# Hybrid conformer and forgetting-attention layer on one core: scores pinned behind maxima in TensorE's order, bias rows stored once, value loads apart, later roots in parts, second block first

## The chip, the cores and the metric

One NeuronCore of a Trainium2 chip runs the whole layer in one launch. The metric is the device time of that launch in microseconds. The engines are TensorE (PE), VectorE (DVE), ScalarE (ACT), GpSimd (POOL) and SyncE (SP), which here issues most of the DMA transfers; POOL issues the others. Each engine takes its own instructions in the order in which the program has them, so an instruction that waits holds up those behind it on its engine.

## The reference

One encoder layer with D_MODEL 1024 for 2048 prompt frames and 8 streams of 16 sample frames; all in float32. Heads are 8 of 64 channels, the convolution group has 512 channels, the FFN 2816.

```python
def _mixer_inputs(x, shift, scale, norm1_g, w_in, b_f, q_norm_g, k_norm_g):
    h = _rmsnorm(x, norm1_g) * (1 + scale) + shift
    u_a, u_g, q, k, v, f = jnp.split(h @ w_in, [...], axis=-1)
    u = u_a * jax.nn.sigmoid(u_g)
    # q and k: RMS norm of each head
    logf = jax.nn.log_sigmoid((f + b_f).astype(jnp.float32))
    return u, q, k, v, logf

def _attend(q, k, v, cum_q, cum_k, q_pos, k_pos):
    s = jnp.einsum('bqhd,bkhd->bhqk', q, k) * (HEAD_DIM ** -0.5)
    s = s + (cum_q[..., :, None] - cum_k[..., None, :])
    s = jnp.where(k_pos[None, :] <= q_pos[:, None], s, NEG_INF)
    p = jax.nn.softmax(s, axis=-1)
    return jnp.einsum('bhqk,bkhd->bqhd', p, v)

def _layer(x, c, past, ...):
    sh1, sc1, g1, sh2, sc2, g2 = _modulation(c, w_ada, b_ada)
    u, q, k, v, logf = _mixer_inputs(x, sh1, sc1, ...)
    # prompt: causal attention; sample: over 1024 cached frames and its own 16
    conv_out = _conv_module(u_hist, conv_w, conv_b, ln_g, ln_b)   # depthwise 31, LayerNorm, swish
    mix = jnp.concatenate([conv_out, attn], axis=-1) @ w_out
    x = x + g1 * mix
    h = _rmsnorm(x, norm2_g) * (1 + sc2) + sh2
    x = x + g2 * ((jax.nn.silu(h @ w_gate) * (h @ w_up)) @ w_down)
    return x, (k, v, logf, new_conv)
```

## The kernel before

Matrix products run as three passes: each operand is split into a rounded part (`hi`, a copy on ACT) and the rest (`lo`, a subtraction on DVE or POOL); `parts_of` does that at lines 1149 and 1150. The stages follow each other, with work of neighbouring stages woven in:

- *Start, 0 to about 120 us.* Modulation (`ada`), then blocks of 384 frames through the input projection. `h_block` loads a block's x, squares it on ACT, makes the root of its mean square (`pr`, L455), and yields the normalised, split `hx` piece by piece. `project_u_v` does the first block while weights `Wu` arrive, then loads and splits the eight pieces of `Wv` (`wraw`, `wvh`, `wvl`), and only after them starts `h_block` of the second block. `pg` and `pa` are the gated products, `pvv` the values.
- *Projection of q and k, to about 600 us*, beside the convolution's taps on DVE. `finish` norms each block (`ssq`, `R`, `qn`, `qp`) and writes `q_d` and `k_d`.
- *Attention, about 600 to 1225 us.* 16 steps, for each of 4 head pairs p and 4 query blocks qb of 512. A step is cut into pieces: 128 keys by up to 512 queries of one head; there are 320 in all. `score_maxima` makes the row maxima beforehand: a matmul `mx` (L927) into one of two `cv` banks, and a reduction `M` on DVE (L930); when a step's maxima are made, `spread_maxima` puts them as extra rows into `Q2`, and it does so after the fourth maximum of the step that follows. `attend` computes each piece's scores `s` (L966, L967) with these rows, the exponential `ef` and its copy `e` on ACT, the subtraction for `e` on DVE (on POOL every third time), and the matmuls `pv` with the values some pieces later. `ef` is a ring of three tiles; `load` takes one of them for a value block `vraw`, which ACT and DVE split into `V`. `load(0)` stands ahead of the first step. `K1`, `K2` are rings of six tiles, `Q2` of four. Beside the steps `background` runs the convolution's LayerNorm (`lane`, `cy`) and the attention of the sample streams.
- *Sample streams.* `sample_setup` makes a bias row of 1040 for each of 64 (stream, head) pairs and stores it 16 times over, once for each query, in `bias_d`; `sample_batch` loads a stream's 128 rows into `S`.
- *Output projection, to 1434 us* (`acc`, L1133), and the *FFN* (`z`, L1440), three pairs of frame blocks by a fast matrix multiplication with seven products of sub-blocks (`sums`, `right_sides`). The first pair's norm lies in `project_out`; those of the second and third are made by `norms` during the first pair of `ffn_up`, one step of the generator for each `q` from the second pair of columns (`f`) on. `root` holds matmuls `pr` (L1229), a chain of small Newton steps on DVE, diagonals `odg` (L1237), matmuls with them (L1238) and a copy to `oR` on ACT.

The order of instructions on each engine is set by a scheduler, which simulates the program and picks by readiness and priority. `weave` sets the order in which a step's parts are handed to it, and `after` binds one instruction behind another of the same engine without a wait:

```python
    def after(self, ins, last):
        self.tc.add_manual_dep(
            ins.ins, last.ins.name,
            mybir.DependencyInfo(mybir.DependencyClass.NoSync, mybir.DependencyReason.DATA), reason="order")
```

## Time and profile before

| | us |
|---|---|
| median of 3 runs (lowest to highest) | 2842.85 (2842.31 to 2846.67) |
| the profiled execution | 2842.93 |
| its span, first to last instruction | 2841.2 |
| PE busy | 2729.4 |
| DVE busy | 2160.8 |
| ACT busy | 1435.3 |
| POOL busy | 506.0 |

In the rows that follow, a table of stretches gives for each its bounds, its length, the busy time of the engines with the number of instructions, the granted TensorE clock as a share of full speed, the DMA engines' share and GB/s. A row of a group gives line, engine, operation, output<-input, shapes and count, then busy us and mean ns, then the engine's idle time just before these instructions and what ended it. A row of a timeline gives start and duration, and in brackets the idle time before it and what ended it. A row of the chain gives start, duration and what. A row of DMA issues ends with the KB of one, and the us to its landing where the profile has it. A row that ends in two numbers behind a name tells who waited, for how many us and how often.

### The profile page before, as it was taken

Reading aid. Unit: us, or ns where it says so; the run is one execution under the profiler, and the core shown is the slowest. Engines: PE = TensorE matmul, PEld = TensorE weight load, DVE = VectorE, ACT = ScalarE, POOL = GpSimd, SP = SyncE. Lnnn points to the kernel's source line nnn. Section 1 sums busy time; section 2 is a strip of 40 time slices with the busy share of each in tenths; the row PEclk is TensorE's granted clock in tenths of the full one; section 3 lists DMA queues with packets and bytes.
Section 4 is the critical chain, followed back from the end, with each engine's and each line's share of the span. In section 5 each row is a group of like instructions: output and inputs, shape, how many; then the busy total and the mean of one; then the engine's idle time right before and its main releaser. Section 6 shows DMA issues by size and latency. Waiting matters only on the chain.

```text
span 2841.2 us, 48479 instructions
## 1 busy us (share of the span) xinstructions
PE 2729.4 (96%) x16536; PEld 2521.3 (89%) x16536; DVE 2160.8 (76%) x4235; ACT 1435.3 (51%) x2812; POOL 506.0 (18%) x685
## 2 busy tenths in 40 slices
PE   7899999989988999999998999999999999999999
PEld 6899988866666777788998999999999999999999
DVE  3698898988786788635488899777797778676765
ACT  4443323357675777754354455444454446555552
POOL 3454411243232222213202020000000000000000
PEclk9999999988899999999998999999999999999999
DMA  8763567674236656355667678776786669788883
GB/s 306 247 196 113 176 220 255 189 204 124 82 110 175 191 182 185 116 174 189 212 238 232 237 264 287 255 229 208 227 296 213 217 209 310 245 281 257 271 255 117
DMA packets 390024, 603.23 MB, mean 212 GB/s; under 512 B 46240, under 2 KB 249152, under 8 KB 387728
## 3 DMA queue, kind: packets, MB, share of 16 engines
q1 hardware_dynamic: 375312, 574.72, 62.6%
q0 software_dynamic: 14464, 25.42, 3.7%
q8 instruction: 130, 2.13, 0.3%
q14 instruction: 118, 0.97, 0.1%
HBM read 421.97 MB, written 178.07 MB: 211 GB/s over the span
## 4 chain that ended last, share of the span: by engine, by line
PE 78%; DMA 9%; DVE 6%; ACT 3%; issue 3%; POOL 2%; SPq 1%; DVEq 0%; ACTq 0%; POOLq 0%
PE z L1440 44%; PE z L510 7%; PE pv L957 5%; PE acc L1133 4%; PE pa L320 3%; PE pvv L340 3%; PE pg L320 3%; PE s L966 2%; PE s L967 2%; PE mx L927 2%; DMA vraw<-o_v 1%; DVE M L930 1%; DMA wraw<-w_in 1%; DMA k_d<-qp 1%; PE lane L1096 1%
## 5 line engine op out<-in xcount | busy, mean ns | idle before, releaser
L1440 PE MATMUL z<-rT,rW 128*128 128x360 f32 (+1 forms) x8316 | 1382.6, 328 | 5.1 <-ACT oR L1240 1.9
L1440 PEld LDWEIGHTS z<-rT,rW 128*128 128x128 f32 x8316 | 1379.4, 188 | 6.9 <-ACT oR L1240 2.3
L1149 ACT ACTIVATE rW<-rR 128x512 fp32r<-128x512 f32 x714 | 435.1, 617 | 397.9 <-PE z L1440 285.6
L1150 DVE TENSOR_TENSOR rW<-rR,rW 128x512 fp32r<-128x512 f32 x714 | 477.6, 673 | 154.7 <-ACT rW L1149 150.8
L698 DVE SCALAR_TENSOR_TENSOR cv<-cu,cpar,cv 128x384 f32<-128x384 f32 x580 | 311.6, 616 | 2.6 <-ACT cv L696 2.5
L957 PE MATMUL pv<-e,V 128*128 128x512 f32 (+3 forms) x960 | 265.0, 381 | 22.6 <-ACT e L1149 13.1
L957 PEld LDWEIGHTS pv<-e,V 128*128 128x128 f32 x960 | 168.9, 192 | 68.3 <-ACT e L1149 15.2
L930 DVE TENSOR_REDUCE M<-mx 128x1 f32<-128x512 f32 (+2 forms) x320 | 190.1, 605 | 50.5 <-PE mx L927 34.9
L971 ACT ACTIVATE ef<-s 128x512 f32<-128x512 f32 (+3 forms) x320 | 166.0, 529 | 104.8 <-PE s L967 46.7
L510 PE MATMUL z<-hqx,wqh 128*128 128x384 f32 (+1 forms) x768 | 196.6, 333 | 1.3 <-DVE logf L347 1.3
L1149 ACT ACTIVATE rT<-traw 128x360 fp32r<-128x360 f32 (+1 forms) x315 | 149.9, 501 | 88.8 <-DMA traw<-gt_d 52.5
L1150 POOL TENSOR_TENSOR e<-ef,e 128x512 fp32r<-128x512 f32 (+3 forms) x106 | 127.0, 1198 | 364.4 <-ACT e L1149 182.1
L1150 DVE TENSOR_TENSOR rT<-traw,rT 128x360 fp32r<-128x360 f32 (+1 forms) x315 | 158.4, 533 | 41.3 <-ACT rT L1149 41.0
L1150 DVE TENSOR_TENSOR e<-ef,e 128x512 fp32r<-128x512 f32 (+3 forms) x214 | 147.3, 698 | 40.8 <-ACT e L1149 38.1
L1149 ACT ACTIVATE e<-ef 128x512 fp32r<-128x512 f32 (+3 forms) x320 | 174.2, 565 | 4.4
L510 PEld LDWEIGHTS z<-hqx,wqh 128*128 128x128 f32 x768 | 135.7, 188 | 19.2 <-issue 15.5
L927 PE MATMUL mx<-K,Q 96*128 96x512 f32 (+2 forms) x320 | 133.6, 426 | 15.3 <-DVE M L930 13.2
L1133 PE MATMUL acc<-ch,woh 128*128 128x360 f32 (+1 forms) x384 | 128.4, 336 | 9.9 <-ACT ch L1149 5.0
L1368 DVE TENSOR_TENSOR rR<-rR 128x512 f32<-128x512 f32 (+1 forms) x136 | 90.5, 683 | 54.6 <-DMA rR<-w_down 50.0
L966 PE MATMUL s<-Q,K 128*128 128x512 f32 (+3 forms) x320 | 126.7, 397 | 3.2 <-ACT ef L971 3.0
L1133 PE MATMUL acc<-ch,wol 128*128 128x360 f32 (+1 forms) x384 | 128.1, 334 | 0.0
L510 PE MATMUL z<-hqx,wql 128*128 128x384 f32 (+1 forms) x384 | 126.4, 329 | 0.0
(306 smaller groups left out, 3955.5 us busy)
## 6 DMA issues: line engine op xcount, KB each, us to landing
rR<-sup_d SPq DMA_DIRECT2D x176, 256.0 KB
rR<-w_gate SPq DMA_DIRECT2D x132, 256.0 KB
traw<-gt_d SPq DMA_DIRECT2D x154, 180.0 KB
rR<-w_down SPq DMA_DIRECT2D x104, 256.0 KB
rR<-sdn_d SPq DMA_DIRECT2D x96, 256.0 KB
rR<-w_up SPq DMA_DIRECT2D x88, 256.0 KB
sup_d<-rR SPq DMA_DIRECT2D x88, 256.0 KB
wa<-w_ada SPq DMA_DIRECT2D x16, 1024.0 KB
```

The source lines that it names most:

```text
L320: nc.tensor.matmul(pz[:, :n], w[:, m], x[:, :n], start=(c == 0 and k == 0), stop=(c == CB - 1 and k == 2))
L510: nc.tensor.matmul(z[:, :n], w[:, m], x[:, :n], start=(c == 0 and k == 0), stop=(c == CB - 1 and k == 2))
L698: self.pin(nc.vector.scalar_tensor_tensor(dst, src, w, acc[i], ALU.mult, ALU.add))
L927: nc.tensor.matmul(mx[:, :w], Q2[0:AUX, h, j * P:(j + 1) * P], K2[kb][0:AUX, h, :w], start=True, stop=not diag)
L930: nc.vector.tensor_reduce(M[:, i, kb:kb + 1], mx[:, :w], AX.X, ALU.max)
L957: nc.tensor.matmul(z[h][:, off:], V[kt // 4][:, v, kt % 4, h:h + 2, :].rearrange("p b c -> p (b c)"), e[:, x, off:], start=(kt == 0 and i ...
L966: nc.tensor.matmul(s[:, off:], K1[kb][:, h, sl], Q1[:, h, off:], start=True, stop=False)
L971: nc.scalar.activation(ef[:, off:], s[:, off:], AF.Exp)
L1133: self.nc.tensor.matmul(z[:, :n], w[:, m], y, start=(first and i == 0 and k == 0), stop=(last and i == len(terms) - 1 and k == 2))
L1149: self.nc.scalar.activation(hi, raw, AF.Copy)
L1150: engine.tensor_tensor(lo, raw, f32(hi), ALU.subtract)
L1440: nc.tensor.matmul(z, W[:, x, m], t[:, y, :w], start=(k == 0 and i == 0), stop=(k == n - 1 and i == 2))
```

## The change

Five things are changed. (1) Every score piece's first matmul is bound behind the maximum that is 32 to 40 pieces on (32 for the first, one more for every six). (2) `bias_d` holds each row once, and `S` is loaded head by head with the row repeated 16 times by the load. (3) `vraw` has a tile of its own tag `rs`, shared with the reciprocal of a step's end, instead of one of the `ef` ring; `load` yields after its transfer is issued, and the split's copy on ACT is bound behind the last exponential written so far; the first block's load is issued ahead of the steps and split among them. (4) `root` yields twice between the diagonals and their matmuls, and `norms` starts at the third pair of columns. (5) `h_block` of the second block starts ahead of the `Wv` loads.

```diff
-            self.bias_d = d.tile([NS * H, QS, PAST + QS], F32, name="bias_d")
+            self.bias_d = d.tile([NS * H, PAST + QS], F32, name="bias_d")
...
         wvp = ctx.enter_context(self.pool(name="wv", bufs=1))
+        pending = None
+        h1 = self.h_block(*BLOCKS1[1], stage, sp, hp)
+        next(h1)
         Wv = [self.split(wvp, 2 * D, 520, c, "wv", nc.vector) for c in range(CB)]
-        pending = None
-        hs_next = list(self.h_block(*BLOCKS1[1], stage, sp, hp))[2:]
+        hs_next = list(h1)[1:]
...
-        drain(self.load(0))
+        first = self.load(0)
+        next(first)
+        next(first)
...
                 parts.append((self.last_parts(), 12))
+                parts.append((first, 4))
...
-        raw = self.awk.tile([P, 4, P], F32, tag="ef", name="vraw", bufs=3)
+        raw = self.awk.tile([P, 4, P], F32, tag="rs", name="vraw", bufs=1)
         nc.sync.dma_start(raw, self.a["o_v"][t].rearrange("(t p) e -> p t e", p=P)[:, :, p * P:(p + 1) * P])
         v = self.Vt[n % 4]
+        self.V.setdefault(p, []).append(v)
+        yield
         hi, lo = (v[:, i, :, 0:3:2, :] for i in range(2))
-        self.parts_of(hi, lo, raw.rearrange("p t (h e) -> p t h e", h=2), nc.vector)
-        self.V.setdefault(p, []).append(v)
+        self.after(self.parts_of(hi, lo, raw.rearrange("p t (h e) -> p t h e", h=2), nc.vector), self.last_piece)
...
+                    self.mx.append(nc.tensor.matmul(mx[:, :w], Q2[0:AUX, h, j * P:(j + 1) * P], K2[kb][0:AUX, h, :w], start=True, stop=not diag))
...
+                first = nc.tensor.matmul(s[:, off:], K1[kb][:, h, sl], Q1[:, h, off:], start=True, stop=False)
+                at = min(self.nscore + AHEAD + min(self.nscore // 6, 8), len(self.mx) - 1)
+                self.after(first, self.mx[at])
+                self.nscore += 1
...
+                self.last_piece = nc.scalar.activation(ef[:, off:], s[:, off:], AF.Exp)
...
-        nc.sync.dma_start(self.bias_d, bias[:n].unsqueeze(1).broadcast_to([n, QS, PAST + QS]))
+        nc.sync.dma_start(self.bias_d, bias[:n])
...
-        nc.sync.dma_start(S, self.bias_d[b * H:(b + 1) * H].rearrange("h q k -> (h q) k"))
+        for h in range(H):
+            nc.sync.dma_start(S[h * QS:(h + 1) * QS], self.bias_d[b * H + h:b * H + h + 1].broadcast_to([QS, PAST + QS]))
...
-                first.append(self.root(*pending, sp))
+                drain(self.root(*pending, sp, first))
...
+        dg = [sp.tile([P, NW // 4], F32, tag="dg", name="odg", bufs=4)[:m, :m] for _ in range(4)]
         for i in range(4):
-            dg = sp.tile([P, NW // 4], F32, tag="dg", name="odg", bufs=4)[:m, :m]
-            nc.vector.tensor_scalar(dg, ident[:m, :m], r[:, i:i + 1], None, ALU.mult)
-            nc.tensor.matmul(pr[:, i * m:(i + 1) * m], ones[:m], dg, start=True, stop=True)
+            nc.vector.tensor_scalar(dg[i], ident[:m, :m], r[:, i:i + 1], None, ALU.mult)
+        yield
+        yield
+        for i in range(4):
+            nc.tensor.matmul(pr[:, i * m:(i + 1) * m], ones[:m], dg[i], start=True, stop=True)
...
-                R.append(self.root(s, n, pool))
                 yield
+                yield from self.root(s, n, pool, R)
...
-                        if p == 0 and f and u == 0:
+                        if p == 0 and f > 2 and u == 0:
                             next(norms, None)
```

Where this stands in the engines' order. The first place is TensorE at the border of the third and fourth step of the first pair: `mx` are maxima, `s` scores, `pv` matmuls with values, `pz` the transposition ahead of `Q2`'s rows. Before:

```order
L966 MATMUL s<-Q_7802,K_6647 128x512
L957 MATMUL pv<-e,V_7013 128x128
L714 MATMUL lane<-cq,ones 32x512
...
L927 MATMUL mx<-K_6643,Q_6667 128x512
L927 MATMUL mx<-K_6648,Q_6667 128x512
L927 MATMUL mx<-K_6655,Q_6667 128x512
L927 MATMUL mx<-K_6658,Q_6667 128x512
L929 MATMUL mx<-masks 128x128
L927 MATMUL mx<-K_6661,Q_6645 128x128
L929 MATMUL mx<-masks 128x128
...
L941 MATMUL pz<-ident,Z_6636 128x128
```

After, at the same `pz`:

```order
L973 MATMUL s<-Q_7440,K_6657 128x384
L977 MATMUL s<-Q_6653,K_6655 128x384
L979 MATMUL s<-masks 128x128
L964 MATMUL pv<-e,V_7013 128x512 x2
L934 MATMUL mx<-K_6661,Q_6645 128x512
L936 MATMUL mx<-masks 128x128
L973 MATMUL s<-Q_7440,K_6657 128x256
L977 MATMUL s<-Q_6653,K_6655 128x256
L979 MATMUL s<-masks 128x128
L948 MATMUL pz<-ident,Z_6636 128x128
```

Before, 14 maxima stand with no score between them ahead of the transposition that the next step needs; after, a maximum and a score alternate, and the scores that are on are still those of the step before.

The second place is SP's order of transfers around the bias store, before:

```order
L1040 DMA bias_d<-bias 1024x1x1040
L901 DMA vraw<-o_v 128x4x128
L1054 DMA kc<-kcT 128x4x512
L1046 DMA S<-bias_d 128x1040 x2
L1054 DMA kc<-kcT 128x4x512
```

and after:

```order
L1050 DMA bias_d<-bias 64x1040
L1065 DMA kc<-kcT 128x4x512
L1057 DMA S<-bias_d 16x1040 x16
L906 DMA vraw<-o_v 128x4x128
L1006 DMA cat_d<-pvs 128x512
```

The value load `vraw` that stood right behind the store now stands ahead of the whole set-up, and the next one behind the sixteen loads of `S`.

The third place is TensorE in the FFN's first pair, around the roots of the second pair, before:

```order
L1440 MATMUL z<-rT,rW 128x368 x264
L1229 MATMUL pr<-sp_13306,ns 90x2 x4
L1440 MATMUL z<-rT,rW 128x368 x72
L1238 MATMUL pr<-odg,sp_13305 128x90 x4
L1229 MATMUL pr<-sp_13306,ns 90x2 x4
L1238 MATMUL pr<-odg,sp_13305 128x90 x4
L1440 MATMUL z<-rT,rW 128x368 x372
```

and after:

```order
L1456 MATMUL z<-rT,rW 128x368 x372
L1241 MATMUL pr<-sp_13362,ns 90x2 x4
L1456 MATMUL z<-rT,rW 128x368 x134
L1253 MATMUL pr<-odg,sp_13361 128x90 x4
L1456 MATMUL z<-rT,rW 128x368 x46
L1241 MATMUL pr<-sp_13362,ns 90x2 x4
L1456 MATMUL z<-rT,rW 128x368 x72
L1253 MATMUL pr<-odg,sp_13361 128x90 x4
```

The two halves of the second root stood together, with no FFN matmul between; now 134 and 72 stand between the halves.

More of the change, by code (lines that the diff above doesn't have):

```diff
@@ L899, in load @@
         self.Q1[n] = Q1
-        raw = self.awk.tile([P, 4, P], F32, tag="ef", name="vraw", bufs=3)
+        raw = self.awk.tile([P, 4, P], F32, tag="rs", name="vraw", bufs=1)
         nc.sync.dma_start(raw, self.a["o_v"][t].rearrange("(t p) e -> p t e", p=P)[:, :, p * P:(p + 1) * P])
         v = self.Vt[n % 4]
+        self.V.setdefault(p, []).append(v)
+        yield
         hi, lo = (v[:, i, :, 0:3:2, :] for i in range(2))
-        self.parts_of(hi, lo, raw.rearrange("p t (h e) -> p t h e", h=2), nc.vector)
-        self.V.setdefault(p, []).append(v)
+        self.after(self.parts_of(hi, lo, raw.rearrange("p t (h e) -> p t h e", h=2), nc.vector), self.last_piece)
     def score_maxima(self):
         nc = self.nc
+        self.mx, self.nscore = [], 0
         spread = None
@@ L926, in score_maxima @@
                     mx = self.bank("cv", "mx")
-                    nc.tensor.matmul(mx[:, :w], Q2[0:AUX, h, j * P:(j + 1) * P], K2[kb][0:AUX, h, :w], start=True, stop=not diag)
+                    self.mx.append(nc.tensor.matmul(mx[:, :w], Q2[0:AUX, h, j * P:(j + 1) * P], K2[kb][0:AUX, h, :w], start=True, stop=not diag))
                     if diag:
@@ L965, in attend @@
                 s = self.bank("u", "s")
-                nc.tensor.matmul(s[:, off:], K1[kb][:, h, sl], Q1[:, h, off:], start=True, stop=False)
+                first = nc.tensor.matmul(s[:, off:], K1[kb][:, h, sl], Q1[:, h, off:], start=True, stop=False)
+                at = min(self.nscore + AHEAD + min(self.nscore // 6, 8), len(self.mx) - 1)
+                self.after(first, self.mx[at])
+                self.nscore += 1
                 nc.tensor.matmul(s[:, off:], K2[kb][:, h, sl], Q2[:, h, off:], start=False, stop=not diag)
@@ L970, in attend @@
                 ef = wk.tile([P, 512], F32, tag="ef", name="ef", bufs=3)
-                nc.scalar.activation(ef[:, off:], s[:, off:], AF.Exp)
+                self.last_piece = nc.scalar.activation(ef[:, off:], s[:, off:], AF.Exp)
                 pool, tag = self.eslots[self.ecount % len(self.eslots)]
@@ L1147, in parts_of @@
     def parts_of(self, hi, lo, raw, engine):
-        self.nc.scalar.activation(hi, raw, AF.Copy)
+        copy = self.nc.scalar.activation(hi, raw, AF.Copy)
         engine.tensor_tensor(lo, raw, f32(hi), ALU.subtract)
+        return copy
     def split_rows(self, hi, lo, src, ring, tag):
@@ L1221, in project_out, with root @@
                 self.pump()
-    def root(self, ssum, n, sp):
+    def root(self, ssum, n, sp, out):
         nc, (ones, mean, ident) = self.nc, self.spread
@@ L1234, in root @@
         newton_rsqrt(nc, r, t, v, 3)
+        dg = [sp.tile([P, NW // 4], F32, tag="dg", name="odg", bufs=4)[:m, :m] for _ in range(4)]
         for i in range(4):
-            dg = sp.tile([P, NW // 4], F32, tag="dg", name="odg", bufs=4)[:m, :m]
-            nc.vector.tensor_scalar(dg, ident[:m, :m], r[:, i:i + 1], None, ALU.mult)
-            nc.tensor.matmul(pr[:, i * m:(i + 1) * m], ones[:m], dg, start=True, stop=True)
+            nc.vector.tensor_scalar(dg[i], ident[:m, :m], r[:, i:i + 1], None, ALU.mult)
[3 more added lines that the diff above has]
+            nc.tensor.matmul(pr[:, i * m:(i + 1) * m], ones[:m], dg[i], start=True, stop=True)
         R = sp.tile([P, NW], F32, tag="R", name="oR", bufs=2)
         nc.scalar.copy(R[:, :n], pr[:, :n])
-        return R
+        out.append(R)
+        yield
     def norm(self, p, pool, x1, R):
```

## The prediction

> **What bounds the kernel now.** I read the engine totals first, then busy time by stage, then the granted clock in the worst places, then the waits inside each.
>
> ```profile
> span 2841.2 us, 48479 instructions
> PE 2729.4 (96%) x16536; PEld 2521.3 (89%) x16536; DVE 2160.8 (76%) x4235; ACT 1435.3 (51%) x2812; POOL 506.0 (18%) x685
> ```
>
> TensorE is busy for 96%, which leaves 112 us of idle time at most, plus what a lowered clock costs. The table by stage (stretch, length, busy us of TensorE, its weight loads, VectorE, ScalarE, GpSimd, then the granted clock) says where:
>
> ```profile
> 0.00:130.00 130.00, 101.48 (x758) 93.19 (x759) 55.72 (x114) 58.90 (x105) 50.13 (x98) 0.93 0.82 281
> 130.00:600.00 470.00, 467.69 (x3011) 427.37 (x3010) 425.34 (x964) 166.59 (x328) 172.54 (x321) 1.00 0.61 193
> 600.00:950.00 350.00, 305.58 (x1361) 218.67 (x1359) 276.07 (x477) 226.40 (x459) 109.44 (x110) 0.89 0.49 138
> 950.00:1225.00 275.00, 263.81 (x1848) 196.60 (x1847) 207.70 (x364) 212.24 (x422) 71.23 (x67) 0.99 0.52 162
> 1225.00:1434.00 209.00, 201.32 (x1190) 199.24 (x1191) 95.58 (x187) 83.33 (x161) 57.26 (x56) 0.98 0.58 189
> 1434.00:1625.00 191.00, 177.75 (x1042) 174.79 (x1041) 168.07 (x354) 89.57 (x175) 25.39 (x23) 0.96 0.73 246
> 1625.00:2841.20 1216.20, 1211.73 (x7336) 1211.42 (x7334) 932.29 (x1782) 598.30 (x1166) 20.00 (x12) 1.00 0.76 244
> ```
>
> The last row, the FFN from its second third on, is full at full clock, and so is 130 to 600; the change can hardly win there. Three stretches have slack: the start (28.5 us idle), the first half of attention (44 us idle, clock 0.89) and the start of the FFN (13 us idle, clock 0.96). The edits fall into these three; the stage 1225 to 1434 keeps its distances between root matmuls and I cost it at nothing.
>
> ```profile
> 728.90:745.90 17.00, 11.47 (x29) 8.09 (x30) 15.44 (x30) 4.59 (x9) 1.17 (x1) 0.50 0.28 95
> 920.00:933.60 13.60, 5.23 (x14) 4.26 (x15) 5.57 (x8) 5.39 (x10) 2.75 (x3) 0.50 0.95 274
> 1496.90:1513.90 17.00, 12.22 (x44) 11.43 (x45) 9.67 (x29) 5.79 (x12) 4.97 (x6) 0.50 0.53 166
> ```
>
> In each of these the granted clock is 0.50. A place where TensorE waits therefore costs the wait and then half of the matmul time in the stretch behind it.
>
> **Second block first (start).**
>
> ```profile
> 75.88 6.58 DMA x<-x
> 85.03 6.06 DMA x<-x
> 84.01 0.58 PE L340 MATMUL pvv<-wvh,hx 128*128 128x260 f32 x1 [2.27 <-ACT v L344]
> 102.04 0.69 PE L320 MATMUL pg<-hx,wuh 128*128 128x384 f32 x1 [4.19 <-ACT hx L471]
> ```
>
> The squares of later blocks' x stand on ScalarE ahead of the copy of `pvv` and of block 1's `hx`, and each waits for its x. After, block 1's three x loads stand ahead of the eight `Wv` loads on SP, and its root matmuls fall into the first two value tiles. Shown gain: 2.3 + 4.2 = 6.5 us of waits, and a few us of half clock. Against it: 1.5 MB of x ahead of `Wv` takes 5.5 us at the 281 GB/s of the first stage's row, and the last `Wv` pieces were only just in time. Bounds: 0 (the delay eats the waits) to 14 us (waits, clock, and the slower hx feed behind them). I take **8**, nearer to the two rows than to zero, since the project_v matmuls cover most of the delay.
>
> **Scores behind maxima, values apart, bias once (attention).** The rows are VectorE's groups from 600 to 950 (busy us, mean ns, idle us before), TensorE's score group, and the score matmuls alone in two stretches:
>
> ```profile
> L930 DVE TENSOR_REDUCE M<-mx 128x1 f32<-128x512 f32 (+3 forms) x183 | 108.6, 603 | 32.8 <-PE mx L927 22.0 <-PE mx L929 9.6
> L1150 DVE TENSOR_TENSOR e<-ef,e 128x512 fp32r<-128x512 f32 (+3 forms) x107 | 73.5, 701 | 12.6 <-ACT e L1149 12.0
> L1150 DVE TENSOR_TENSOR V<-vraw,V 128x512 fp32r<-128x512 f32 x9 | 6.6, 732 | 17.2 <-ACT V L1149 17.2
> L966 PE MATMUL s<-Q,K 128*128 128x512 f32 (+3 forms) x166 | 67.6, 407 | 2.1 <-ACT ef L971 2.0
> 667.50:683.00 15.50, 0.05 (x1) 0.18 (x1) 0.89 0.27 71
> 718.90:742.60 23.70, 0.04 (x1) 0.04 (x1) 0.71 0.26 83
> 739.63 0.48 PE L927 MATMUL mx<-K,Q 96*128 96x128 f32 x1 [2.53 <-DVE M L930]
>   PE mx L927: 13.2, 21
> ```
>
> For 15.5 and 23.7 us no score starts: TensorE issues maxima alone, two banks deep, and waits for reductions on VectorE (the last row: 13.2 us in 21 waits, 0.63 each), and ScalarE starves. In TensorE's order a score stood 13 to 37 maxima behind the newest one, falling and then jumping; after, it stands 33 and then a steady 41 or so, until the maxima run out. The need (a step's bias rows come four maxima into the next step) is 36 at the widest, so the jumps go.
>
> VectorE is the engine nearest its limit here: 276 of 350 us. No maximum or subtraction is removed, so the floor is its work: 276 + 10 more maxima pulled in front of score 166 (lead 41 for about 31) x 0.603 = 282 us. Of its 74 us idle, 17.2 wait for the values' copy, 32.8 for maxima, 12.6 for `e`, 11 for the rest. The first goes (value loads no longer stand in the exp ring or at the head of ScalarE), the second I halve (reductions come alternately with subtractions, so a bank has time to refill), the others stay: 40. Then 282 + 40 = 322 instead of 350, a gain of 28. From 950 on TensorE is 264 of 275 busy; ten maxima less at about 0.23 us each start to start give 2 back, and the first score, which now waits for 33 maxima instead of 14, I charge with 3 (what is done meanwhile is needed anyway). Sum **27**. Bounds: 50, if VectorE idles only for `e` and the rest (282 + 24 = 306, less the same 6 us of doubt); minus 15, if the halving fails and the later first score (20 maxima x 0.603 = 12 us, and a few) isn't earned back.
>
> Part of the 27 is the bias store:
>
> ```profile
> bias_d<-bias SPq DMA_DIRECT2D x1, 4160.0 KB
> 902.14 25.00 DMA vraw<-o_v
> 927.17 0.63 ACT L1149 ACTIVATE V<-vraw 128x512 fp32r<-128x512 f32 x1 [12.45 <-DMA vraw<-o_v]
> 928.37 0.80 PE L957 MATMUL pv<-e,V 128*128 128x512 f32 x1 [10.36 <-ACT e L1149]
> 924.68 0.81 SPq L1046 DMA_DIRECT2D S<-bias_d  x2
> ```
>
> 4160 KB go out ahead of a 256 KB value load, which takes 25 us; ScalarE stands 12.45 us, TensorE 10.36, and the clock halves behind it. After, 260 KB are stored. The reads keep their bytes but become 64 issues for 8: 56 x 0.4 = 23 us of SP's time over some 290 us, behind which value loads and `cat_d` stores queue; they are issued most of a step early, which covers it. The Trainium skill (DMA: Bandwidth & Descriptors, Rules for kernel authors) speaks against this split: many small transfers should be one large one, since under 64 KB one pays mostly overhead; these are 65 KB. With about 2 us for each (same page), 56 in a row would be an estimated 112 us, and the sum above would turn into a loss of some 60; that page's price holds only if they run one behind the other and on the path, which no run here shows yet.
>
> On the clock: the Trainium skill (TensorE: Matmul & The Clock Gate, HAM oscillation) lets the clock fall after idle gaps over about 3.4 us. The 10.36 us wait agrees. In 728.9 to 745.9 the clock is 0.50 although the longest wait shown is 2.53 us; there the trace decides. By the rule alone only the gaps of `vraw` and of the start would give clock back, an attention gain of about 15 for 27, close to the first rival below.
>
> **Later roots in parts (FFN).** Stretches of 168 FFN matmuls each:
>
> ```profile
> 1462.90:1504.30 41.40, 28.58 (x170) 27.99 (x168) 0.91 0.63 208
> 1504.40:1537.30 32.90, 32.34 (x168) 31.86 (x169) 0.86 0.68 226
> 1537.40:1565.40 28.00, 28.00 (x170) 28.00 (x169) 1.00 0.89 287
> 1565.50:1597.60 32.10, 28.74 (x170) 27.88 (x168) 1.00 0.87 297
> 1597.80:1629.30 31.50, 28.66 (x168) 28.06 (x169) 1.00 0.46 158
> 1495.11 1.13 PE L1238 MATMUL pr<-odg,sp 90*128 90x90 f32 x8 [3.21 <-DVE odg L1237]
> 1500.97 2.02 PE L1238 MATMUL pr<-odg,sp 90*128 90x90 f32 x8 [2.83 <-DVE odg L1237]
> ```
>
> Undisturbed, one takes 28.0; four take 137.9 for 112, so 26 us are lost where the roots stand. TensorE comes to the diagonal matmul while VectorE still works through the small Newton steps. After, 46 to 134 FFN matmuls (0.167 us each, 8 to 22 us) stand between a root's halves, more than the chain needs, and the next call comes 72 later. Starting at the third pair of columns moves the same work and is covered by the ring. Bounds: 6 (the two waits shown) to 26. I take **15**: the waits and the half clock go, while GpSimd's and ScalarE's `nx` work on the same calls stays.
>
> **Sum.** 8 + 27 + 15 = 50. The profiled execution took 2842.93 us (span 2841.2 and 1.7 around it), 0.1 from the median of the runs, 2842.85. 2842.9 - 50 = **2793 us**.
>
> **Rivals.** *Stalls alone* (20%): VectorE already bounds attention and the burst only hid its queue; then the value copies' 17 less 5 for the later start remain, 12 in attention: 8 + 12 + 15 = 35, 2808 us. For it: in 728.9 to 745.9 VectorE is busy 15.4 of 17. Against: the 32.8 us idle before reductions.
>
> *More* (15%): attention at its bound, 50, with 8 + 17: 2768 us.
>
> *Operands late* (8%):
>
> ```profile
> K<-k_d POOLq DMA_DIRECT2D x16, 512.0 KB, 5.5
> L966 PE MATMUL s<-Q,K x320: 220/393/796, 614.1 to 1215.1; 128*128 128x512 f32 x112, 128*128 128x384 f32 x16, 128*128 128x256 f32 x16, 128*128 128x128 f32 x16
> ```
>
> With the maxima 41 ahead, a pair's third key block and fourth query block reuse buffers that a score frees only some 8 pieces before; at 1.88 us a piece (601 us for 320) that is 15 us for a GpSimd issue and a 5.5 us landing. It fits; with GpSimd late, six such places at 5 us cost 30: 2823 us.
>
> *Slower* (8%): each of some 280 pinned scores now stands behind a maximum, and that behind a reduction; ScalarE's exp starves whenever VectorE works on anything else. If half of them wait what the burst's waits last, 0.6 us, that is 84 us against the 35 of the first rival: 2892 us. It decides from 35 / 280 = 0.125 us a score. For it: two banks only; against: one maximum a score needs a bank each 1.88 us, and a reduction takes 0.6.
>
> *Small loads on the path* (4%): value loads and stores wait for the split `S` loads, at the 0.4 us that SP spends on one: 23 of the 50 are lost, 2816 us. Against: they are issued early. The skill's page on DMA, above, is the case for it.
>
> *Nothing moves* (5%): the waits go and return as VectorE time; within 0.2% (5.7 us, about what a measurement of this kernel can tell).
>
> **How the numbers follow.** 40% for the forecast (its own range 2780 to 2805), and the rivals as given. Faster 0.40 + 0.20 + 0.15 + 0.08 + 0.04 = 0.87, same 0.05, slower 0.08. The range 2764 to 2828 reaches from the upper rival to late operands and leaves out some 15%.
>
> **What would show it.** Right: no wait over 3 us on `vraw`; score matmuls in every 15 us stretch from the first on; granted clock over 0.95 and VectorE over 85% in the first 320 us of attention; every 168 FFN matmuls near 28 us; `pg` of block 1 some 10 us earlier. Wrong: TensorE waits for M growing well over 13 us, maxima waiting for K or Q loads, or `pvv` waiting for `wvl`.

## The result, and the profile after

| | before | after |
|---|---|---|
| median of 4 runs each, us | 2842.58 | 2818.45 (2814.3 to 2821.02) |
| ratio, 95% interval | | 0.9913 (0.9894 to 0.9932) |
| the profiled execution's span, us | 2841.2 | 2812.5 |

The change wins 24 us; 50 were forecast. The profiled execution of after is the fastest of its four, so its trace shows 28.7 us of gain. They lie as follows, by the start of the first matmul of each stage in the two traces:

| stage | forecast | in the traces |
|---|---|---|
| start, up to the projection of q and k | 8 | 6.9 (353.1, now 346.2) |
| from there to the output projection (attention) | 27 | 18.5 (872.8, now 854.3) |
| output projection | 0 | 0.4 (207.1, now 206.7) |
| FFN | 15 | 2.8, all of it in the first 3360 matmuls (585.4, now 582.6) |

The page's totals of after, and the table by stage at shifted bounds (columns as in the prediction: stretch, length, busy us of PE, PEld, DVE, ACT, POOL, granted clock, DMA share, GB/s):

```profile
span 2812.5 us, 48566 instructions
PE 2718.6 (97%) x16536; PEld 2515.7 (89%) x16536; DVE 2161.9 (77%) x4235; ACT 1428.7 (51%) x2812; POOL 503.9 (18%) x685
0.00:123.40 123.40, 100.48 (x758) 92.64 (x759) 55.84 (x114) 58.13 (x105) 51.16 (x98) 0.94 0.86 295
593.00:925.00 332.00, 304.99 (x1369) 218.62 (x1368) 279.39 (x488) 227.95 (x462) 111.58 (x111) 0.92 0.45 124
925.00:1199.50 274.50, 256.55 (x1841) 194.52 (x1840) 202.25 (x351) 205.72 (x417) 68.56 (x66) 0.98 0.59 171
1408.00:1599.00 191.00, 186.01 (x1109) 184.35 (x1108) 171.84 (x338) 94.20 (x183) 23.37 (x19) 0.98 0.75 247
```

No work went: the instruction counts of the engines are those of before, VectorE's busy time is the same within 1.1 us, and TensorE's falls by 10.8 us with less of it at half clock. The first half of attention, 350 us before for about the same 1365 TensorE instructions, takes 332; 322 were forecast. The first FFN stretch still has clock 0.98 and 5 us idle.

**Start.** The two waits of before (2.27 and 4.19 us) read after:

```profile
89.55 0.39 PE L340 MATMUL pvv<-wvh,hx 128*128 128x260 f32 x1 [3.11 <-ACT v L344]
103.07 0.44 PE L320 MATMUL pg<-hx,wuh 128*128 128x384 f32 x1 [1.52 <-ACT hx L473]
```

The first has grown, the second shrunk; together they fall by 1.8 us only. The second block's products begin at 99.8 for 102.0, its values at 136.6 for 143.1, and the stage as a whole ends 6.9 us earlier. So 4.4 of the 6.9 us come between these two points, where the shown waits do not stand.

**Attention.** VectorE's groups from 593 to 925, TensorE's longest waits there, and the score matmuls alone in stretches placed like the two scoreless ones of before:

```profile
L937 DVE TENSOR_REDUCE M<-mx 128x1 f32<-128x512 f32 (+2 forms) x198 | 116.7, 602 | 37.9 <-PE mx L934 22.5 <-PE mx L936 14.5
L1161 DVE TENSOR_TENSOR e<-ef,e 128x512 fp32r<-128x512 f32 (+3 forms) x109 | 74.6, 688 | 8.7 <-ACT e L1160 8.3
L1161 DVE TENSOR_TENSOR V<-vraw,V 128x512 fp32r<-128x512 f32 x9 | 6.3, 704 | 0.0
PE mx L934 <- DVE M L937: 7.3, 11, 1.4
PE pv L964 <- DVE e L1161: 5.6, 12, 1.1
652.00:667.50 15.50, 1.76 (x7) 1.14 (x6) 1.00 0.42 132
700.00:724.00 24.00, 4.77 (x13) 2.48 (x13) 1.00 0.31 96
```

The scoreless stretches are gone: 7 and 13 scores stand where there were one each. The longest time between two `s` matmuls is 6.7 us, where before it was 21.9. The 17.2 us that VectorE stood idle ahead of `V` are gone too. The 32.8 us ahead of the maxima, which the forecast halved, became 37.9 (0.18 us a maximum before, 0.19 after).

**FFN.** The waits at roots, and the stretch of 168 matmuls around the second root of the second pair:

```profile
PE pr L1253 <- DVE odg L1249: 5.0, 2, 2.6
1493.20:1530.90 37.70, 33.85 (x194) 32.82 (x194) 26.82 (x64) 15.12 (x28) 6.06 (x7) 0.91 0.46 150
1517.55 1.83 PE L1253 MATMUL pr<-odg,sp 90*128 90x90 f32 x8 [2.58 <-DVE odg L1249]
1519.92 4.05 PE L1456 MATMUL z<-rT,rW 128*128 128x368 f32 x12 [0.55 <-ACT oR L1255]
1640.99 2.02 PE L1253 MATMUL pr<-odg,sp 90*128 90x90 f32 x8 [2.39 <-DVE odg L1249]
```

The first root of each of the two pairs does not stall TensorE now; each second root still does, and its stretch takes 37.7 and 38.7 us for 28. The blocks of 168 are in a row 29.0, 28.1, 28.8, 37.7, 28.0, 28.9, 28.8, 38.7, 29.8, 27.9.

### The profile page after: what moved, and what is told of

Read it like the earlier page. It is cut to its first block, busy times and chain, and to the rows that moved or that the text cites. A ratio compares the mean times of both kernels' runs of the same rounds, so it can differ in the third digit from the quotient of the medians.

```text
span 2812.5 us, 48566 instructions
## 1 busy us (share of the span) xinstructions
PE 2718.6 (97%) x16536; PEld 2515.7 (89%) x16536; DVE 2161.9 (77%) x4235; ACT 1428.7 (51%) x2812; POOL 503.9 (18%) x685
```

## Experiments

Each kernel was timed against the kernel before on the same chip. "Attention" is, in the profiled execution, the time from the first matmul of the q and k projection to the first of the output projection; "FFN" that of the first 3360 FFN matmuls. Attention differs by up to 5 us between kernels whose attention is the same (854.3 to 859.2 for after, skip, joint and noss), and FFN by 4; smaller differences are not read. The medians come from several chips; kernels are compared by their ratios.

| run | median (range, runs) | ratio (95% interval) | attention | FFN |
|---|---|---|---|---|
| before | | 1 | 872.8 | 585.4 |
| after | 2818.45 (2814.3 to 2821.0, 4) | 0.9913 (0.9894 to 0.9932) | 854.3 | 582.6 |
| pin_off | 2834.4 (2831.8 to 2842.4, 12) | 0.9988 (0.9976 to 0.9999) | 876.9 | 581.7 |
| pin_only | 2825.27 (2821.5 to 2833.8, 6) | 0.9946 (0.9932 to 0.9960) | 853.0 | 583.9 |
| vals | 2809.97 (2802.0 to 2813.2, 6) | 0.9894 (0.9876 to 0.9912) | 853.5 | 583.2 |
| bias | 2818.95 (2817.1 to 2825.8, 6) | 0.9931 (0.9914 to 0.9948) | 857.7 | 584.7 |
| one | 2818.25 (2813.3 to 2829.2, 6) | 0.9929 (0.9910 to 0.9949) | 857.7 | 584.8 |
| ramp | 2814.08 (2805.9 to 2823.3, 6) | 0.9912 (0.9896 to 0.9927) | 858.4 | 580.9 |
| gps | 2815.65 (2812.2 to 2822.3, 6) | 0.9919 (0.9901 to 0.9936) | 853.9 | 582.5 |
| pair | 2815.59 (2813.1 to 2818.5, 4) | 0.9906 (0.9877 to 0.9936) | 856.3 | 582.8 |
| pv2 | 2790.86 (2784.9 to 2794.0, 4) | 0.9820 (0.9792 to 0.9848) | 827.2 | 581.5 |
| skip | 2807.48 (2804.7 to 2813.1, 4) | 0.9890 (0.9877 to 0.9903) | 858.0 | 570.4 |
| joint | 2816.97 (2811.1 to 2820.8, 5) | 0.9922 (0.9908 to 0.9935) | 859.2 | 583.5 |
| noss | 2811.85 (2811.5 to 2814.6, 4) | 0.9898 (0.9885 to 0.9911) | 858.6 | 573.9 |
| best | 2811.57 (2809.7 to 2816.0, 4) | 0.9900 (0.9885 to 0.9915) | 857.5 | 577.1 |
| best2 | 2803.79 (2802.3 to 2805.8, 4) | 0.9875 (0.9859 to 0.9892) | 851.0 | 573.1 |

### The roots: distance against chain

**skip.** The second root's halves three calls farther apart (`apart` is 2 for a pair's first root, 5 for its second), and the bank of an open root left out of the FFN products' rotation. The edit in part:

```diff
-        yield
-        yield
+        for _ in range(apart):
+            yield
...
+        if self.open_root and BANK8[self.nbank % 8] == "ss":
+            self.nbank += 1
```

> The changed kernel, with the halves of the second root of each pair three calls farther apart (94 and 100 FFN matmuls between them instead of 72), and with the bank of the open root left out of the rotation of products. Theory (the FFN lost its share because the Newton chain on VectorE, 13 us with what is interleaved, is longer than the 12 us of FFN matmuls behind which the second root's second half stands): the two waits of 2.6 and 2.4 us on odg and the half clock behind them go; each of the two blocks of 37.7 and 38.7 us falls to 28 to 30; 2818 becomes 2800 (2796 to 2806). Rival (the loss comes from the work of the same calls, nx, right sides and the rings, and shows up wherever the root stands): the blocks stay near 38 us, 2814 to 2820.

The waits of TensorE at the roots in the trace of this run:

```profile
PE pr L1241 <- DVE eU L1486: 3.4, 1, 3.4
```

No wait on `odg` is left. The two blocks of 37.7 and 38.7 us take 29.6 and 30.6, and FFN 570.4, 12 us less than after, as the theory says. One new wait of 3.4 us stands ahead of a root's first half, whose bank an FFN product still held; its block takes 34.0. The median stays above the 2796 to 2806 expected, and by the ratios the whole gains 6.5 us on after: the new wait takes some 6 us, and attention in this run is 4 us longer than in the profile of after. That the distance removes the waits, and not the bank, is seen in pin_off below, which has no edit at the roots. Its order gives the second pair's second root 72 matmuls again, and TensorE waits 2.6 us; the third pair's second root happens to get 84, and there it does not wait:

```profile
1650.69 14.26 PE L1455 MATMUL z<-rT,rW 128*128 128x368 f32 x84
1664.78 1.02 PE L1252 MATMUL pr<-odg,sp 90*128 90x90 f32 x8
```

What makes the chain so long is seen in after, in VectorE's timeline: the first and the last link of the second root's chain are 13.2 us apart.

```profile
1504.06 0.15 DVE L1243 TENSOR_SCALAR ov<-pr 90x4 f32<-90x4 f32 x1
1517.23 0.79 DVE L1249 TENSOR_SCALAR odg<-sp,or 90x90 f32<-90x90 f32 x4
```

The twelve steps from `ov` to the last one ahead of `odg` take 0.15 us each. In VectorE's order one to six operations of 0.5 to 0.7 us for other tiles (`rW`, `rR`, `eU`, `et`) stand between every two of the first steps. 72 FFN matmuls at 0.167 us are 12 us, less than this. In the kernel before, VectorE's order had the same twelve steps of the second pair's second root in a row, and they took 2.5 us:

```profile
1498.17 0.16 DVE L1231 TENSOR_SCALAR ov<-pr 90x4 f32<-90x4 f32 x1 [1.36 <-PE pr L1229]
1500.65 0.79 DVE L1237 TENSOR_SCALAR odg<-sp,or 90x90 f32<-90x90 f32 x4
```

**joint.** One Newton chain with eight columns for both roots of a pair.

```diff
-            for h in range(2):
-                s = pool.tile([P, NW], F32, tag="ns", name="ns", bufs=1)
-                nc.sync.dma_start(s[:, :n], self.r_d[2 * p + h, :, :n])
-                yield
-                yield from self.root(s, n, pool, R)
+            yield from self.roots(p, n, pool, R)
```

(`roots` is new: both sums, one chain, then two sets of diagonals with their matmuls.)

> The changed kernel, with one Newton chain for both roots of a pair (eight columns instead of four), 103 and 116 FFN matmuls ahead of the first diagonal matmuls and 48 and 36 ahead of the second. Theory (chain length against distance): no wait on odg over 0.5 us, blocks at 28 to 30 us, 2799 (2795 to 2806), and a little under the run with the halves farther apart, since half of the small VectorE steps are gone. Rival (other work of the calls): 2812 to 2820.

```profile
1606.53 1.38 PE L1270 MATMUL pr<-sp,ns 128*90 128x2 f32 x8 [5.72 <-DMA ns<-r_d]
1636.61 1.13 PE L1285 MATMUL pr<-odg,sp 90*128 90x90 f32 x8 [0.47 <-DVE eV L1515]
```

On `odg` the theory holds: no wait over 0.5 us. But the load of the third pair's second sum, one call ahead of its matmuls, comes too late by 5.7 us, and blocks of 32.2, 37.8 and 32.4 us turn up; FFN is where it was. A stall removed here was replaced by another of its size.

**noss.** The roots' bank left out of the rotation of the FFN products until the last pair is normed, `apart` as in skip; 153 and 112 matmuls between the halves of the second roots. The edit in part:

```diff
+        if self.normed < len(PAIRS) and BANK8[self.nbank % 8] == "ss":
+            self.nbank += 1
```

> The changed kernel with 153 and 112 FFN matmuls between the halves of the pairs' second roots and the roots' bank left out of the products' rotation until the last pair is normed. Theory (distance of the second half, and with the bank kept free also the wait of 3.4 us that the run with three calls more still showed ahead of a root's first half): no wait over 1 us at a root, every block of 168 matmuls under 30 us, the first 3360 in 563 (560 to 567) for 583, the whole 2796 (2792 to 2801). Rival (seven banks instead of eight make products wait for their evacuation, or the rings run dry elsewhere): blocks of 30 to 35 us at other places, 570 or more, 2803 to 2812.

```profile
1605.44 13.80 PE L1458 MATMUL z<-rT,rW 128*128 128x368 f32 x81
1623.37 2.02 PE L1253 MATMUL pr<-odg,sp 90*128 90x90 f32 x8 [4.14 <-DVE odg L1249]
1650.45 1.02 PE L1253 MATMUL pr<-odg,sp 90*128 90x90 f32 x8
```

At the second roots, with 153 and 112 matmuls, nothing waits (the last row). The wait of 4.1 us stands at the third pair's first root, which the new order left with 81 matmuls, 13.5 us, where after has 134. From its first half to its second 18.5 us pass, although 84 matmuls sufficed in pin_off: the chain's length is not fixed, it depends on what VectorE's order puts between its steps. FFN takes 573.9 and the whole 2811.85, where the rival has them, but the stall is at a root again and not at the seven banks.

### Attention: which part carries it

**pin_off.** After without the pin.

```diff
-                self.after(first, self.mx[at])
```

> The changed kernel without the pin of the scores behind maxima; values apart, the bias stored once, the start and the roots stay. Theory (the pin takes the bursts of maxima away and is the larger part of attention's gain): stretches of 15 to 24 us without a score come back between 640 and 720, from the q and k projection to the output projection attention takes 866 (862 to 870) where the changed kernel takes 854 to 859, and the whole 2824 (2820 to 2830). Rival (values and bias carry it, and the order of scores only moves work about): attention 855 to 860, the whole 2812 to 2819.

```profile
655.50:671.50 16.00, 0.42 (x2) 0.00 (x0) 0.89 0.35 106
707.00:725.70 18.70, 0.44 (x1) 0.19 (x1) 0.82 0.24 69
```

These are the score matmuls alone, as in the prediction: the scoreless stretches of 16.0 and 18.7 us are back, and attention takes 876.9, more than the theory's 870. Values apart and the bias stored once bring nothing to attention without the pin; with the start and the roots still in it, the whole is 0.1% faster than before.

**pin_only.** The kernel before with the pin alone.

> The kernel before with the pin of the scores alone; first block, value loads, bias store and roots as before. Theory (the pin carries attention's gain, values and bias add nothing beside it): attention 857 (852 to 861) for 873 before, the whole 2823 (2818 to 2828), although ScalarE waits for value loads as before. Rival (pin and values or bias only pay together: behind a pin the 12 us wait for the value load at the bias store stops the scores as well): attention 866 to 873, a wait of 8 us or more at the store, 2831 to 2840.

Attention takes 853.0, as in after. The output projection behind it takes 214.8 us for 207.1, so that up to the FFN 12.2 of the 19.8 us are left; other kernels with the pin take 206.0 to 213.4 there. ScalarE still waits for value loads, and the bias store costs one wait:

```profile
950.16 0.80 PE L967 MATMUL s<-Q,K 128*128 128x512 f32 x1 [7.42 <-ACT ef L975]
```

**vals.** After with the value loads as before.

```diff
-        raw = self.awk.tile([P, 4, P], F32, tag="rs", name="vraw", bufs=1)
+        raw = self.awk.tile([P, 4, P], F32, tag="ef", name="vraw", bufs=3)
```

(The yield, the binding of the copy and the early first load are undone with it.)

> The changed kernel with the value loads back in the ring of the exponentials, and the first of them made ahead of attention. Theory (17 us of VectorE's idle time ahead of V, gone after, was time on the path): VectorE's idle time ahead of V is back at 10 to 17 us in the first half of attention, attention 864 to 870, the whole 2823 (2819 to 2829). Rival (most of that wait was the burst of the bias store, which stays away, so the place of the loads matters little): wait on vraw under 5 us in all, attention 855 to 860, the whole 2812 to 2819.

```profile
L1157 DVE TENSOR_TENSOR V<-vraw,V 128x512 fp32r<-128x512 f32 x9 | 7.4, 827 | 0.9 <-ACT V L1156 0.9
```

The idle time ahead of `V` stays away though the loads are back, and the kernel is no slower. So the 17.2 us did not hang on the place of the loads. Most of them, 11.65 us, stood before at the one value block that landed behind the bias store, as the rival has it:

```profile
927.83 0.69 DVE L1150 TENSOR_TENSOR V<-vraw,V 128x512 fp32r<-128x512 f32 x1 [11.65 <-ACT V L1149]
```

ScalarE still waits for `vraw` here, 22 us in all of attention where the rival allows 5, and the time does not show it.

**bias.** After with the bias stored 16 times, and `S` loaded by one transfer again. The edit in part:

```diff
-        nc.sync.dma_start(self.bias_d, bias[:n])
+        nc.sync.dma_start(self.bias_d, bias[:n].unsqueeze(1).broadcast_to([n, QS, PAST + QS]))
```

> The changed kernel with the bias stored 16 times over (4160 KB) and read by one load a batch, as before. Theory (the store's traffic delays what lies behind it on SP and in the DMA engines): K and Q loads of GpSimd and one value load land 10 to 20 us later, a wait of 6 to 12 us at 915 to 945 with half clock behind it, attention 864 to 872, the whole 2826 (2820 to 2832). Rival (the changed kernel pays the same at S, 2.8 and 4.1 us of waits and 7 us of half clock, so the store once only changes who waits): attention within 4 us, 2815 to 2821.

```profile
949.39 0.63 ACT L1159 ACTIVATE V<-vraw 128x512 fp32r<-128x512 f32 x1 [12.19 <-DMA vraw<-o_v]
950.06 0.69 DVE L1160 TENSOR_TENSOR V<-vraw,V 128x512 fp32r<-128x512 f32 x1 [11.11 <-ACT V L1159]
951.06 5.00 PE L964 MATMUL pv<-e,V 128*128 128x512 f32 x13 [11.71 <-ACT pvs L999]
```

The waits come back in full on all three engines, at 949 where before they stood at 927, much as the theory says. Yet attention is only 3 us longer than in the profile of after, no longer than in skip, joint and noss, where the rival has it. By the ratios storing once is worth 5 us (0.9931 against 0.9913), but the intervals overlap: from nothing to some 12 us fits them.

**one.** After with one transfer for a batch's `S`.

```diff
-        for h in range(H):
-            nc.sync.dma_start(S[h * QS:(h + 1) * QS], self.bias_d[b * H + h:b * H + h + 1].broadcast_to([QS, PAST + QS]))
+        nc.sync.dma_start(S, self.bias_d[b * H:(b + 1) * H].unsqueeze(1).broadcast_to([H, QS, PAST + QS]))
```

> The changed kernel with the bias read by one transfer a batch, which repeats each row 16 times at its source, instead of eight of 65 KB. Theory (the split loads cost 14.7 us of SP's time at 925 to 940, and the first lane matmul and a value load stood behind them): the 4.1 us wait on S and what half clock follows go, 3 to 6 us less: 2814 (2811 to 2817), SP's time for S under 5 us in all. Rival (SP's time is covered, the batch waits for the stored bias anyway): 2817 to 2821, with the wait on S still there.

SP's first issues and the first lane matmul, of after and then of this run:

```profile
925.29 14.70 SPq L1057 DMA_DIRECT2D S<-bias_d  x16
940.53 1.60 PE L1073 MATMUL lane<-kc,Qbd 128*32 128x512 f32 x8 [4.12 <-DVE S L1075]
```

```profile
922.93 1.34 SPq L1056 DMA_DIRECT2D S<-bias_d  x2
938.19 1.78 PE L1072 MATMUL lane<-kc,Qbd 128*32 128x512 f32 x8 [4.07 <-DVE S L1074]
```

SP is free after 1.3 us instead of 14.7, and the matmul waits just as long. The rival is right: the split is covered. Here the Trainium skill (DMA: Bandwidth & Descriptors, Rules for kernel authors), which would join small transfers into one, is not borne out in time: joined or split, the times can't be told apart (0.9929 and 0.9913, intervals overlapping).

### What sets the time of the first half now

**ramp.** A smaller lead at the start.

```diff
-                at = min(self.nscore + AHEAD + min(self.nscore // 6, 8), len(self.mx) - 1)
+                at = min(self.nscore + 13 + min(self.nscore // 2, 27), len(self.mx) - 1)
```

> The changed kernel with the first score behind maximum 13 instead of 32, the lead growing by one for every two scores until it is 40. Theory (the later first score, 17 us behind the start's gain where 3 were charged, is part of the missing attention gain): first score 10 to 17 us earlier, no half clock of 34 us at the start of attention, the first accumulation of the output projection 6 to 10 us earlier: 2810 (2806 to 2814). Rival (VectorE bounds these 100 us, and whatever it does first, the sum of its work sets the end): score 60 and the projection where they were, within 2 us, 2816 to 2821.

The first score comes at 603.8 for 624.6, half clock there is 27 us for 34, and score 60 starts at 734.4 for 733.6 (the stage began 1.3 us later). The rival is right: within these 2 us a first score some 20 us later costs nothing.

**gps.** Every second subtraction on GpSimd.

```diff
-                self.split3 = (self.split3 + 1) % 3
+                self.split3 = (self.split3 + 1) % 2
```

> The changed kernel with every second subtraction of attention's pieces on GpSimd instead of every third; 53 of them leave VectorE, some 37 us of its busy time, 20 of it in the first half. Theory (VectorE bounds the first half of attention: busy 279 of 332 us, and its idle time ahead of M is only order): the first half gets 8 to 15 us shorter, attention 845 (840 to 850), the whole 2804 (2798 to 2810). Rival (the two engines take turns at two banks, and TensorE's order sets the time; a piece on GpSimd takes 1.2 us for 0.7 and delays its value matmuls): attention within 4 us or longer, waits of pv on GpSimd up from 2.3 us to 5 or more, 2812 to 2825.

VectorE has a quarter fewer subtractions in the first half, but its time in them falls by 9 us only and not by 20 (65.5 for 74.6), since those that stay are longer, 809 ns for 688. Its idle time ahead of the maxima stays where it was:

```profile
L937 DVE TENSOR_REDUCE M<-mx 128x1 f32<-128x512 f32 (+3 forms) x196 | 116.0, 604 | 38.7 <-PE mx L934 27.7 <-PE mx L936 10.3
L1161 DVE TENSOR_TENSOR e<-ef,e 128x512 fp32r<-128x512 f32 (+1 forms) x81 | 65.5, 809 | 5.4 <-ACT e L1160 5.3
```

Attention is the same. So 9 us less of VectorE's work buys nothing there. The cost that the rival named did not come either: TensorE's waits for subtractions on GpSimd are 3.1 us for 2.3.

**pair.** Both scores of a key tile behind the same maximum.

```diff
-                at = min(self.nscore + AHEAD + min(self.nscore // 6, 8), len(self.mx) - 1)
+                at = min(self.nscore + AHEAD + min(self.nscore // 6, 8) + 1 - h, len(self.mx) - 1)
```

> The changed kernel with the two scores of a key tile pinned behind the same maximum, so that two maxima and two scores alternate instead of one and one. Theory (turns at two banks cost time: with two maxima in a row VectorE has both banks to reduce while TensorE issues two scores): VectorE's idle time ahead of M in the first half falls from 37 us to 25 or less and attention by 4 to 10 us. Rival (the idle time ahead of M is only VectorE waiting for its place in TensorE's order): idle ahead of M within 5 us, attention within 3 us.

The idle time ahead of `M` is 36.9 us for 37.9, and attention the same: the rival, as far as alternating two and two can show it.

**pv2.** A third of the value matmuls left out.

```diff
-            for i, (v, x) in enumerate(((0, 0), (0, 1), (1, 0))):
+            for i, (v, x) in enumerate(((0, 0), (0, 1))):
```

> The changed kernel without the third of the value matmuls that take the values' lower part (320 of 960; the result lacks that part). Some 47 us of TensorE's 306 busy us between 593 and 925 go, and some 43 of the 257 up to the output projection. Theory (after the pin, TensorE's own work with its order sets attention's time): attention shrinks by more than 70 of the 90 us, in both halves. Rival (in the first half VectorE, or the turns of TensorE and VectorE at two banks, set the time): the first half shrinks by less than 20, the second by 30 or more.

From the first maximum to score 160 the time falls by 20.2 us, from there to the output projection by 7.7. The stretches of after and of this run, first half and then second:

```profile
578.30:917.90 339.60, 312.59 (x1442) 226.96 (x1442) 289.07 (x519) 231.51 (x466) 115.36 (x116) 0.92 0.45 124
580.10:899.50 319.40, 288.33 (x1250) 198.79 (x1250) 287.66 (x500) 228.98 (x466) 115.05 (x114) 0.91 0.43 117
917.90:1200.50 282.60, 263.65 (x1888) 200.22 (x1886) 206.87 (x360) 212.93 (x430) 72.06 (x71) 0.98 0.60 175
899.50:1174.40 274.90, 245.51 (x1685) 176.65 (x1683) 207.19 (x376) 211.59 (x429) 76.50 (x73) 0.94 0.68 196
```

The 47 and 43 us expected to go were too much, since matmuls overlap: TensorE's busy time falls by 24.3 and 18.1 us. In the first half 20.2 of these 24.3 us are won, so there TensorE's work in its order carries most of the time. VectorE's idle time ahead of the maxima, 37.9 us up to 925, is 20.1 in the shortened stretch (593 to 910). In the second half only 7.7 of 18.1 are won; the granted clock there is 0.94 for 0.98. By their numbers neither the theory (over 70 us) nor the rival (under 20, then 30 or more) is met. Of the four changes only less work on TensorE shortened attention, which points to TensorE in the first half. ScalarE was not tried, and what bounds the second half stays open.

### A faster version

**best** is noss with the value loads of vals.

> The run with the roots' bank left out of the rotation, and the value loads back in the ring of the exponentials. Theory: the gains add (nothing to 5 us from the values, 16 to 20 from the roots): 2793 (2788 to 2800). Rival (the values' place was noise): the time of the run without it, within 3 us.

It is as fast as noss: the rival.

**best2** is best with the joint chain, each sum loaded two calls ahead of its matmuls, and the first diagonal matmuls four calls behind the chain.

> The changed kernel with the value loads back in the ring of the exponentials, the roots' bank left out of the rotation until the last pair is normed, and one Newton chain for both roots of a pair, its sums loaded two calls ahead, its first diagonal matmuls four calls behind. Theory (what is left at the roots is chain against distance and the late load, each seen in one of the runs before): no wait over 1.5 us at a root, the first 3360 FFN matmuls in 563 to 568 us for 570 with the halves farther apart, the whole 2798 (2793 to 2804). Rival (a chain of small steps in VectorE's order is as late as that order makes it, and a wait of 3 to 5 us with its half clock turns up at the second pair again): 572 to 578, 2805 to 2812.

```profile
1421.75 7.77 PE L1483 MATMUL z<-rT,rW 128*128 128x368 f32 x36 [1.74 <-ACT eU L1502]
1700.67 34.15 PE L1483 MATMUL z<-rT,rW 128*128 128x368 f32 x192 [2.33 <-DVE eV L1514]
```

No wait stands at a root any more. Two others are left, at the FFN's start and 280 us later; FFN takes 573.1, so the waits went as the theory says, FFN lies where the rival has it, and the whole is just inside the theory's 2793 to 2804. At 2803.79 us, ratio 0.9875 (0.9859 to 0.9892) to before, it has the lowest ratio of the kernels that compute everything, with an interval just below that of after.

## Why the prediction was wrong

**The roots (15 forecast, 2.8 measured).** The mechanism and the size were right, the distance was not. The step that failed is "46 to 134 FFN matmuls (0.167 us each, 8 to 22 us) stand between a root's halves, more than the chain needs". The 46 stand between two roots; between the halves stand 134 at each pair's first root and 72, 12 us, at its second, whose chain takes 13.2 us. I had the counts from the order of TensorE and never held them against the chain's length on VectorE. The row for it stood in the prediction: TensorE came to the diagonal matmul while VectorE "still works through the small Newton steps". The 2.8 us measured are no more than what FFN differs by between like kernels; pin_only, with the roots of before, has 583.9. Once the chain fits, skip and best2 win 15.0 and 12.3 us against before, the forecast's term. The price of a missed root is of the kind that the prediction named, the wait and then half clock: 2.6 us of wait, 6.8 us at half clock behind it, and some 8 us in all against the same block of skip (37.7, there 29.6).

**Attention (27 forecast, 18.5 in the trace; 13.7 to 21.9 in the other kernels that keep the pin and all of the work).** The sum was made of VectorE's idle time, row by row, and "the second I halve" failed: ahead of the maxima 16.4 us were forecast for the first half and 37.9 measured. The other terms came out a little better than forecast (`e` and the rest 14.7 us for 23.6, busy 279.4 for 282), which leaves 332 us for 322. "The first goes", the 17.2 us ahead of `V`, came true in the row but was not worth its size: 11.65 of them went with the bias store and not with the place of the loads, and bias brings 11.1 back with attention at 857.7. The pin carries the gain. pin_off shows that without it nothing is left, and pin_only wins 19.8 us in attention with loads and bias store untouched. Some of that can be lost again behind it: up to the FFN the kernels with the pin and all of the work win 9 to 19 us. That the later first score costs little was right for the wrong size: it came 17 us late against the start's gain, not 3 us, and ramp shows that this is free.

**Bias store (a part of the 27).** ScalarE's 12.45 us and TensorE's 10.36 us are gone. In their place, at the same point of the work, TensorE waits 2.8 us for `Q` and 4.1 us for `S` with 6.8 us at half clock. Undone, it costs 5 us by the ratios, too little to tell from nothing. SP's 64 loads of `S` take 28 us themselves, 0.44 each where 0.4 was taken, and 38 us with the pauses between them, one of which lasts 6 us (928.5 to 934.5).

**Start (8 forecast, 6.9 measured).** A gain is there, but its size came near the forecast partly by luck. The two waits that the term was read from fall by 1.8 us, and `pg` of the second block comes 2.2 us earlier and not 10. What is won steadily is the stretch from the second block's first products to its values: 36.2 to 38.9 us in the fourteen traces of kernels with this part, 41.1 and 41.5 in the two without. The projection of q and k begins at 341.8 to 347.5 us in the fourteen, at 348.5 and 353.1 in the two, which have the same start and differ by 4.6. No run undoes this part alone.

**Output projection (0).** It holds in after, 0.4; but other kernels that leave it alone take 205.5 to 214.8 us there, and why is open.

**The rivals.** *Small loads on the path* (2816) gave the nearest number for the whole, by luck: one load a batch wins nothing. *Stalls alone* (2808) gave the nearest for attention, 12, but its cause does not hold: the value copies' 17 us carry nothing, the pin does. *Operands late* showed once, 2.8 us on `Q`. *Slower* did not occur, the pin gains where it had it lose; nor did *More* and *Nothing moves*.

**Of what was to show it:** score matmuls in every 15 us stretch, yes. Clock over 0.95 in the first 320 us, no, 0.92, with 34 us at half clock where maxima stand alone. VectorE over 85% there: 271 of 320 us, 84.8%, just short of it. No wait over 3 us on `vraw`: on TensorE none, ScalarE has one of 4.4. Every 168 FFN matmuls near 28 us: two blocks not, 37.7 and 38.7, and skip, which brings them to 29.6 and 30.6, has the missing 12 us. Of the signs of being wrong, TensorE's waits for `M` fell to 7.3 us, and maxima waited for `Q` once.

## What to carry to other kernels

A pair of halves with "work between" is worth its gain only if the work between is longer than the chain, counted on the engine that runs the chain and with everything that its order puts between the links; a dozen steps of 0.15 us took 13 us here, and 2.5 where nothing stood between them. Idle time ahead of an instruction is not a price for what ended it: undo or make that one edit alone before adding such rows up. And where an order in bursts is the cause, binding two streams one to one can carry the gain, while the waits that looked like its parts may be worth less than a measurement can tell.

## What the runs showed of the hardware

The clock fell to half without a long wait. In after, TensorE runs at 0.50 from 599.6 to 633.7, although it is busy 30.1 of 34.1 us and its longest wait there is 0.85 us:

```profile
599.60:633.70 34.10, 30.12 (x68) 18.00 (x69) 26.85 (x51) 13.20 (x31) 15.49 (x18) 0.50 0.70 187
621.71 0.55 PE L934 MATMUL mx<-K,Q 96*128 96x256 f32 x1 [0.85 <-DVE Q L950]
```

The Trainium skill (TensorE: Matmul & The Clock Gate, A second HAM failure mode) tells of a kernel whose clock went up and down because TensorE paused for short times between groups as it went through its result banks. Waits under 1 us, 4 us in all, at two banks of maxima, agree with that; the rule of gaps over 3.4 us, which the prediction weighed, does not cover it. No run here changes the banks, so the cause stays unproven.

Loads landed late where the DMA engines were nearly full. Around the sample streams' first loads (915 to 945) the packets of SP's and GpSimd's queues take 59.7% and 39.0% of the 16 engines' time, and GpSimd's `K` and `Q` loads take 9.7 to 14.7 us to land:

```profile
Q<-q_d POOLq DMA_DIRECT2D x2, 512.0 KB, 9.7
K<-k_d POOLq DMA_DIRECT2D x1, 264.0 KB, 14.7
```

The prediction took 5.5 us from the median of all. In the run with one `S` load a batch they take 10.1 to 14.8, so the split is not the reason; that the full engines are is likely, not tried.
